# A second whole ring tile at the first block's end, more raw tiles around topk, and the last norm of blocks 2 and 3 written ahead of the gathered block's last selection

## The chip, the cores and the metric

One Trainium2 chip, one core of it. The metric is the device time of one execution in microseconds; lower is better. The times shown are of separate executions on the chip, the median of three.

## What is computed

One layer on 512 tokens of width 2048, all in float32: a mixer of a chunked mLSTM and a forgetting attention with a common output projection, a cross attention to 256 memory rows, and a PEER feed-forward, each with a residual and a layer norm. The reference, cut to what the change touches:

```python
def reference(x, mem, ...):
    h = hybrid_mixer(x, w_in, ..., w_out)
    x = layer_norm(DN_ALPHA * x + h, ln_w[0], ln_b[0])
    h = memory_cross_attention(x, mem, w_xq, w_xkv, w_xo)
    x = layer_norm(DN_ALPHA * x + h, ln_w[1], ln_b[1])
    h = peer_ffn(x, peer_wq, peer_sub_keys, peer_u, peer_v)
    return layer_norm(DN_ALPHA * x + h, ln_w[2], ln_b[2])

def peer_ffn(x, w_pq, sub_keys, expert_u, expert_v):        # cut
    q = (x @ w_pq).reshape(B, S, 8, 2, 128)
    sc = einsum('bshpd,hpnd->bshpn', q, sub_keys)           # two times 128 scores a head
    top_s, top_i = top_k(sc, 16)
    ...                                                     # the best 16 of 16 x 16 sums
    idx, g = ..., softmax(best_s)                           # 128 experts of 16384 for each token
    a = einsum('tkd,td->tk', expert_u[idx], x)
    return einsum('tk,tkd->td', gelu(a) * g, expert_v[idx])
```

## The kernel before

**Blocks.** The tokens are cut in four blocks of 128. Block 0 goes through the mixer alone, blocks 1 to 3 together. After the mixer, block 1 (e1 in the code) and blocks 2 and 3 (e2, two blocks at once) go their own ways through attention and norms. In the PEER part blocks 0 and 1 take the gathered way: a selection (Choice) finds the 128 experts of each token, their rows are gathered by GpSimd's indirect DMA, and VectorE multiplies them in (job_u, line 1027, and job_v, line 1043, one instruction of 128x2048 a job, 256 jobs a block). Blocks 2 and 3 take the dense way: all 16384 experts are multiplied, and a gate matrix G, zero but for the chosen experts, masks them.

**Weights, raw tiles and the ring.** Every weight arrives as a raw tile of 128x2048 floats (1 MB), loaded by SP (load_raw, line 158) from a list of pools in turn (raws["pools"]; two buffers of a pool, one for a pool named "one"). A float32 product is made of float32r parts: ScalarE casts the raw tile to its high part (line 179, two casts of 128x1024), VectorE subtracts it for the low part (line 182), and both land in a ring tile that TensorE reads. With one ring tile it is used as two halves: a cast, a subtract of 128x1024, and the matmuls of half a raw. With two or more, a whole tile is filled at a time (subtract of 128x2048). The second is added while the first block runs (pool wx) and taken away at that block's end; another is added (pool w2) when the mixer of blocks 1 to 3 is done. Lines 201, 243, 244 and 251 are the matmuls of group_ws and group_as that read the ring.

**What sets the order.** The program is written as generators that mix() weaves together, so many steps of one for a step of the other; a scheduler with its own timeline then sets the final order on each engine. Engines run their rows in order, SP's transfers among them.

**Jobs.** Each subtract of the ring is a tick. It adds rate x cost x mult to a credit (at most 2.0), and each whole unit starts one job: the gather is issued, and its VectorE product is placed "lag" ticks later. The rate is set as the jobs left divided by a number (980 for block 1's 256 jobs). The cost is 4.2 for a uT tile and 4 for most others there. mult is 0.7 until topk ends, then 1.3, and 1.0 in main.

**The stretches that the change touches**, in the order of the program:

- The end of the first block: its norm, attention, residual with Bv, second norm and selection (pool pick0) are woven with the first groups of the mLSTM of blocks 1 to 3 (ml1). The ring has one tile in halves here.
- pick1: block 1's selection, woven with the attention of e2 (att). A selection has four groups; a group multiplies by peer_wq, evaluates scores (line 983), copies them (985) and runs select on VectorE (lines 900 to 942); soften (950 to 953) follows the last, and indices writes ei and gg (993, 994), on which the gathers wait. Then block 1's jobs are added, and the second residual (lines 758, 759) and norm of e2 follow: the sum of the statistics (767), rstd (267 to 273), line 770, the scaling on ScalarE (777), PE's transposes (787), and the splits Xh and Xl (147, 148).
- topk: the selection of blocks 2 and 3, eight selects, woven with next_a. One next_a loads a tile of uT, multiplies it by the tokens (lines 1263, 1266, 1270) and, for each pair, applies gelu (ga).
- gbuild: the selections are transposed (line 1304), G is built (L1322 is its matmul) and written to DRAM (gd), with one next_a in every second step.
- The tail of look-ahead: next_a until LOOK tiles are done (64). A pair too far ahead to be kept is spilled to DRAM (gad).
- main: stage_o multiplies vD tiles (lines 1374, 1375, 1383) by hp, the product of G (line 1341 reads it from gd, line 1344 the spilled ga from gad, on SP) and gelu; next_a goes on inside it until all 128 tiles of uT are done. In its second part a third raw tile (pool main) is used.

## Time and profile before

| | us |
|---|---|
| median of 3 executions | 4734.93 (4732.48 to 4737.19) |
| the profiled execution's own time | 4737.65 |
| span of the profiled execution | 4736.0 |
| TensorE busy | 4501.5 |
| VectorE busy | 3766.3 |
| ScalarE busy | 2239.5 |
| GpSimd busy | 885.8 |

The mean granted clock of TensorE is 0.98. The stretches above lie in the trace as follows, counted from the span's start: the first block's end 947 to 1245 us, the last part of pick1 and e2's residual 2850 to 2958, its norm to 3000, topk to 3264, gbuild to 3470, the look-ahead to 3611, and main to 4716. A window's row gives its busy time by engine; a busy TensorE may still run at a lowered clock, so the granted clock is read beside it. A wait's row reads "engine line waited for <- engine line that released it: total us, times, longest". A matmul's listed duration overlaps with its neighbours', so the pace is read from the starts.

### The profile page before, as it was taken

To read this page: it belongs to the slowest core of one execution; us is meant where nothing else is said; L and a number is where in the kernel's file an instruction comes from. 1 tells how busy PE (TensorE), PEld (TensorE's weight loads), DVE (VectorE), ACT (ScalarE), POOL (GpSimd) and SP (SyncE) were. 2 spreads that over 40 slices of the span, in tenths; PEclk is the share of its full clock that TensorE was granted. 3 is DMA by queue.
4 is the path that set the end of the run, shared out by engine and by line. 5 is a ranking of instruction groups with operands and counts; after the bars stand their busy time and mean duration, and the time that the engine had idled before them with its cause. 6 is when DMAs were issued, how large, how long until landed. Compare 5 with 4: busy or idle time off the path is not lost.

```text
span 4736.0 us, 65181 instructions
## 1 busy us (share of the span) xinstructions
PE 4501.5 (95%) x25662; PEld 4001.0 (84%) x25662; DVE 3766.3 (80%) x4276; ACT 2239.5 (47%) x3043; POOL 885.8 (19%) x631
## 2 busy tenths in 40 slices
PE   8999999988999999999999988998979999999998
PEld 6888888888888899999898776898867778888887
DVE  7876777556888877888788669899868998888885
ACT  6766776544334423333323674435743433343333
POOL 1000000000122222222121000212223123333320
PEclk9999999999999999999999999999989999999999
DMA  7899888655798888888699765777899999999994
GB/s 286 323 332 329 321 321 332 226 198 202 272 342 325 333 325 348 333 335 319 257 347 340 261 224 197 290 299 273 333 357 365 409 393 387 379 381 380 381 376 152
DMA packets 260628, 1489.76 MB, mean 315 GB/s; under 512 B 27068, under 2 KB 69116, under 8 KB 91744
## 3 DMA queue, kind: packets, MB, share of 16 engines
q1 hardware_dynamic: 167280, 890.04, 50.6%
q0 software_dynamic: 81664, 561.95, 30.7%
q10 hardware_dynamic: 11376, 33.59, 1.8%
q8 instruction: 201, 3.29, 0.3%
q14 instruction: 107, 0.88, 0.0%
HBM read 1426.72 MB, written 58.76 MB: 314 GB/s over the span
## 4 chain that ended last, share of the span: by engine, by line
PE 59%; DVE 11%; DMA 6%; ACT 3%; issue 2%; ACTq 0%; DVEq 0%; SPq 0%
PE mm L201 19%; PE mm L244 5%; PE mm L243 5%; PE mm L251 5%; DVE ring L182 5%; PE mm L1383 4%; PE mm L1374 4%; PE mm L1375 3%; PE pa L1270 3%; PE pa L1263 3%; PE pa L1266 3%; DVE rows L1027 1%; ACT ring L179 1%; DMA raw<-in_uT 1%; DMA rows<-in_peer_u,ei 1%
## 5 line engine op out<-in xcount | busy, mean ns | idle before, releaser
L179 ACT CAST ring<-raw 128x1024 fp32r<-128x1024 f32 x1568 | 1597.9, 1050 | 1726.6 <-PE mm L201 463.4
L182 DVE TENSOR_TENSOR ring<-raw,ring 128x2048 fp32r<-128x2048 f32 (+1 forms) x968 | 1818.2, 1882 | 586.1 <-ACT ring L179 267.3
L1007 POOL DMA_INDIRECT rows<-in_peer_u,ei x256 | 385.7, 1507 | 1665.6 <-DVE rows L1027 641.6
L201 PE MATMUL mm<-Ah,ring 128*128 128x384 f32 x2560 | 675.3, 343 | 22.5 <-ACT ring L179 12.2
L1007 POOL DMA_INDIRECT rows<-in_peer_v,ei x256 | 433.4, 1693 | 957.2 <-DVE x2l L1043 740.3
L1043 DVE SCALAR_TENSOR_TENSOR x2l<-rows,dots,x2l 128x2048 f32<-128x2048 f32 x256 | 600.4, 2345 | 10.5 <-DMA rows<-in_peer_v,ei 10.1
L1027 DVE SCALAR_TENSOR_TENSOR rows<-rows,x2l 128x2048 f32<-128x2048 f32 x256 | 583.3, 2283 | 27.0 <-DMA rows<-in_peer_u,ei 27.0
L1263 PE MATMUL pa<-Xh,ring 128*128 128x256 f32 x2048 | 504.4, 287 | 48.1 <-ACT ring L179 47.9
L1266 PE MATMUL pa<-Xl,ring 128*128 128x256 f32 x2048 | 499.9, 284 | 0.0
L201 PEld LDWEIGHTS mm<-Ah,ring 128*128 128x128 f32 x2560 | 466.7, 190 | 31.6 <-ACT ring L179 15.7
L1263 PEld LDWEIGHTS pa<-Xh,ring 128*128 128x128 f32 x2048 | 393.5, 192 | 55.5 <-ACT ring L179 53.1
L201 PE MATMUL mm<-Al,ring 128*128 128x384 f32 x1280 | 433.8, 343 | 0.3 <-DVE Al L148 0.3
L1374 PE MATMUL mm<-ring,hph 128*128 128x512 f32 x1024 | 405.2, 396 | 11.3 <-ACT ring L179 10.2
L1375 PE MATMUL mm<-ring,hpl 128*128 128x512 f32 x1024 | 402.7, 394 | 0.0
L1266 PEld LDWEIGHTS pa<-Xl,ring 128*128 128x128 f32 x2048 | 394.2, 192 | 2.1
L243 PE MATMUL mm<-ring,Zh 128*128 128x512 f32 x832 | 328.6, 395 | 5.8 <-ACT ring L179 5.8
L244 PE MATMUL mm<-ring,Zl 128*128 128x512 f32 x832 | 328.9, 395 | 0.0
L243 PE MATMUL mm<-ring,Ah 128*128 128x512 f32 x768 | 306.9, 400 | 1.1 <-ACT ring L179 1.1
L244 PE MATMUL mm<-ring,Al 128*128 128x512 f32 x768 | 304.1, 396 | 0.0
L1270 PE MATMUL pa<-Xh,ring 128*128 128x256 f32 x2048 | 267.2, 283 | 6.8 <-DVE ring L182 6.5
L201 PE MATMUL mm<-Bh,ring 128*128 128x384 f32 x1024 | 262.4, 338 | 4.9 <-ACT ring L179 4.2
L1383 PE MATMUL mm<-ring,hph 128*128 128x512 f32 x1024 | 258.8, 394 | 8.1 <-DVE ring L182 8.1
(388 smaller groups left out, 7100.4 us busy)
## 6 DMA issues: line engine op xcount, KB each, us to landing
raw<-in_w_in SPq DMA_DIRECT2D x256, 1024.0 KB, 6.9
raw<-in_uT SPq DMA_DIRECT2D x128, 1024.0 KB, 7.2
raw<-in_vD SPq DMA_DIRECT2D x128, 1024.0 KB, 9.1
raw<-in_w_out SPq DMA_DIRECT2D x48, 1024.0 KB, 5.7
raw<-in_peer_wq SPq DMA_DIRECT2D x48, 1024.0 KB, 4.9
raw<-in_w_xkv SPq DMA_DIRECT2D x32, 1024.0 KB, 6.6
raw<-in_w_br_ml SPq DMA_DIRECT2D x32, 1024.0 KB, 7.1
raw<-in_w_br_fx SPq DMA_DIRECT2D x32, 1024.0 KB, 6.6
```

Of the source, the lines that this page charges most:

```text
L179: x = nc.scalar.copy(hi[:, c:c + 1024], src[:, c:c + 1024])
L182: s = nc.vector.tensor_sub(lo, src, hi.bitcast(F32))
L201: i = nc.tensor.matmul(o, w, x, start=start and s % per == 0, stop=stop and s % per == per - 1)
L243: nc.tensor.matmul(banks[t], xh[:, tt], wh[:, c], start=k == 0, stop=False)
L244: nc.tensor.matmul(banks[t], xl[:, tt], wh[:, c], start=False, stop=False)
L1007: i = nc.gpsimd.indirect_dma_start(out=rows, out_offset=None, in_=I[table], in_offset=bass.IndirectOffsetOnAxis(ap=ei[t][:, k:k + 1], axis=0))
L1027: i = nc.vector.scalar_tensor_tensor(rows, rows, 1.0, tok[t]["x2l"], op0=ALU.mult, op1=ALU.mult, accum_out=d[:, k % GB:k % GB + 1])
L1043: i = nc.vector.scalar_tensor_tensor(acc, rows, d[:, GB + k % GB:GB + k % GB + 1], acc, op0=ALU.mult, op1=ALU.add)
L1263: i = nc.tensor.matmul(bank, uh[:, sl], xh, start=k == 0, stop=False)
L1266: nc.tensor.matmul(bank, uh[:, sl], xl, start=False, stop=False)
L1374: nc.tensor.matmul(banks[t][g], a[:, tt], vh[:, gs_], start=c == c0, stop=False)
L1375: nc.tensor.matmul(banks[t][g], b[:, tt], vh[:, gs_], start=False, stop=False)
```

## The change

It has five parts.

1. **Ring.** A third ring tile (pool wr0) is added when fx0 of the first block has closed. At that block's end only the tile of wx goes, so that from ml1's first groups to the end of pick0 two whole ring tiles stand where one in halves did. After pick0 the added one goes. Choice takes a "lean" form there (one buffer less each of keysT, qT and sc), and in Ends the rows of x share three "f" buffers with the norm, where "row" had two and "f" two.
2. **Block 1's last selection.** pick1 is run by hand: 15 steps with the attention woven in, then the rest of the attention, then the residual of e2 woven with the last five steps, then its norm, and behind it the last select and soften. Adding block 1's jobs moves behind all of that; the mult after it is 0.5, which was 0.7.
3. **Raw tiles.** From that point a second pool (rw) and in topk a single one (gap) bring the raw tiles to five, two from rw and one from gap beside wp's two. From gbuild on there are three (wp and gap), where there were two until the second part of main and three from there.
4. **topk and gbuild.** In topk's eighth step five next_a run in place of seven; the other two stand behind the copies of the first transposed selection in gbuild.
5. **LOOK** is 68, which was 64: four more uT tiles are multiplied ahead of main, and 28 pairs are spilled, which were 26.

```diff
--- before.py
+++ after.py
@@ -42,7 +42,7 @@
 
 J = 16
 GB = 8
-LOOK = 64
+LOOK = 68
 GA = 7
 MIX = 4
 
@@ -169,7 +169,7 @@
             for i in range(1 if wide else 2):
                 ring["n"] += 1
                 if wide:
-                    t = ring["tiles"][ring["n"] % 2]
+                    t = ring["tiles"][ring["n"] % len(ring["tiles"])]
                     hi, lo, src = t[:, 0:2048], t[:, 2048:4096], raw
                 else:
                     t, o = ring["tiles"][0], (ring["n"] % 2) * 1024
@@ -749,7 +749,7 @@
                 for g in range(4):
                     def ev(t, b, g=g):
                         if first:
-                            xr = self.t("row", 2)
+                            xr = self.t("f", 3)
                             rows = slice((self.b0 + t) * P, (self.b0 + t + 1) * P)
                             self.ld.dma_start(xr, I["x"][rows, g * 512:(g + 1) * 512])
                             r[t][g] = self.rp.tile([P, 512], F32, tag="r", bufs=4 * nb, name=nm("r"))
...
@@ -888,8 +888,8 @@
 
         class Choice:
 
-            def __init__(self, pl, tp, nb):
-                self.tp, self.nb = tp, nb
+            def __init__(self, pl, tp, nb, lean=False):
+                self.tp, self.nb, self.lean = tp, nb, lean
                 self.sel = {n: [pl.tile([P, P], F32, tag=f"{n}{t}", name=nm(f"sel_{n}{t}")) for t in range(nb)]
                             for n in ("i0", "i1")}
                 self.gates = pl.tile([P, nb, P], F32, tag="g2", name=nm("sel_g"))
@@ -956,14 +956,14 @@
                 tp, nb = self.tp, self.nb
                 for g in range(4):
                     qT = {}
-                    ks = tp.tile([P, 4, P], F32, tag="keysT", bufs=2, name=nm("keysT"))
+                    ks = tp.tile([P, 4, P], F32, tag="keysT", bufs=2 - self.lean, name=nm("keysT"))
                     ld.dma_start(ks, I["keysT"][:, 4 * g:4 * g + 4])
 
                     def ev_q(b, bank, qT=qT):
-                        t = tp.tile([P, 512], F32, tag="qT", bufs=3, name=nm("qT"))
+                        t = tp.tile([P, 512], F32, tag="qT", bufs=3 - self.lean, name=nm("qT"))
...
@@ -1108,6 +1108,8 @@
                 yield from ml0(mp, hT, m0)
             with pool("fx0") as fp:
                 yield from fx0(fp, yT, m0, G0)
+            e["wr"] = ExitStack()
+            add_ring(e["wr"].enter_context(pool("wr0")))
             e["xs"] = ExitStack()
             e["x"] = Ends(e["xs"].enter_context(pool("xa0")), 0, 1, nc.gpsimd, nc.gpsimd)
             yield from e["x"].residual(G0, I["w_out"], True)
@@ -1134,7 +1136,7 @@
             mix(e["x"].attend(X1, pr0, PT), ms, 1)
             drain(ms)
         wx.close()
-        del raws["pools"][1:], ring["tiles"][1:]
+        del raws["pools"][1:], ring["tiles"][1]
         ms_.close()
 
         big = ExitStack()
@@ -1177,9 +1179,11 @@
         e["xs"].close()
         take(ml, 2)
         with pool("pick0") as pp:
-            c = Choice(pp, pp, 1)
+            c = Choice(pp, pp, 1, True)
             mix(c.run(X2, nc.gpsimd), ml, 2)
             c.indices(0)
+        del ring["tiles"][1:]
+        e["wr"].close()
         r0s.close()
         gat["pool"] = ctx.enter_context(pool("gat"))
         hp_.append(bs.enter_context(pool("bigB")))
@@ -1223,19 +1227,29 @@
         take(att, 2)
         with pool("pick1") as pp:
             c = Choice(pp, pp, 1)
-            mix(c.run(X2b, nc.sync), att, 5)
+            cr = c.run(X2b, nc.sync)
+            for i in range(15):
+                next(cr)
+                if i % 5 == 4:
+                    take(att, 1)
+            drain(att)
+            cs.close()
+            fpl = ctx.enter_context(pool("x2c", side="right"))
+            mix(e2.residual(PTc, Bv, False), (next(cr) for _ in range(5)), 1)
+            e2.norm(1, X2, lambda: pair(fpl, "X", 16), True)
+            next(cr, 0)
             c.indices(1)
-        drain(att)
-        cs.close()
-        fpl = ctx.enter_context(pool("x2c", side="right"))
+        pre = ExitStack()
+        pp = pre.enter_context(pool("pre", side="right"))
+        rws = ExitStack()
+        rw = rws.enter_context(pool("rw", side="right"))
+        raws["pools"] = [wp, rw]
         while state["done"] < len(jobs):
             raise RuntimeError(f"{len(jobs) - state['done']} jobs left")
         add_jobs(1)
         state["lag"] = 2
         set_rate(980.0)
-        state["mult"] = 0.7
-        drain(e2.residual(PTc, Bv, False))
-        e2.norm(1, X2, lambda: pair(fpl, "X", 16), True)
+        state["mult"] = 0.5
         xs.close()
         bb.close()
 
@@ -1277,17 +1291,18 @@
                 else:
                     gas[c // 2] = ga
 
-        pre = ExitStack()
-        pp = pre.enter_context(pool("pre", side="right"))
+        raws["pools"], raws["one"] = [wp, rw, wp, rw, gap], gap
         with pool("topk", side="right") as tp:
             c = Choice(pp, tp, 2)
             steps = 0
             for w in c.run(X2, nc.sync):
                 if w:
                     steps += 1
-                    for _ in range(7 if steps == 8 else 3):
+                    for _ in range(5 if steps == 8 else 3):
                         next_a(w[1])
         sel = c.sel
+        rws.close()
+        raws["pools"] = [wp, gap, wp]
         state["mult"] = 1.3
 
         def o_bank():
@@ -1304,6 +1319,9 @@
                 nc.tensor.transpose(bank[:, j * P:(j + 1) * P], sel[n][t], ident)
             for j, n in enumerate(("i0", "i1", "g")):
                 nc.vector.tensor_copy(selT[n][:, tt], bank[:, j * P:(j + 1) * P])
+            if t == 0:
+                next_a()
+                next_a()
             for half in range(2):
                 stage = [gp.tile([P, 64, 64], F32, tag="stage", bufs=3, name=nm("stage")) for _ in range(2)]
                 for q in range(16):
@@ -1355,8 +1373,6 @@
         def stage_o(c0, dh, fill):
 
             banks = [[o_bank() for g in range(2)] for t in range(HB)]
-            if c0 == 0 and dh:
-                raws["pools"], raws["one"] = [wp, mn, wp], mn
             for jj in range(J // 2):
                 raw = load_raw(I["vD"][c0 // 2 + jj, dh])
                 for vh, vl, o, w in shares(raw, 2.0):
```

Line numbers behind the changes move by 14 to 18: next_a's 1263, 1266 and 1270 are 1277, 1280 and 1284 after, 1304 is 1319, 1322 is 1340, 1341 and 1344 are 1359 and 1362, 1374 is 1390.

**VectorE at the first block's end.** The rows where the residual of the first block (758, 759) meets ml1's first groups; ring_105 is the ring tile that is always there. Before:

```order
L182 TENSOR_TENSOR ring_105<-raw_7876,ring_105 128x1024 x2
L182 TENSOR_TENSOR ring_105<-raw_7894,ring_105 128x1024 x2
L758 SCALAR_TENSOR_TENSOR r_6278<-r_6278,mm_7875 128x512
L759 BN_STATS rst_7874<-r_6278 128x6
L182 TENSOR_TENSOR ring_105<-raw_7914,ring_105 128x1024 x2
L148 TENSOR_TENSOR Al_7921<-raw_7918,Ah_7920 128x384
L148 TENSOR_TENSOR Al_7925<-raw_7918,Ah_7924 128x384
L148 TENSOR_TENSOR Al_7929<-raw_7918,Ah_7928 128x384
L148 TENSOR_TENSOR Al_7933<-raw_7918,Ah_7932 128x384
```

After, at the same place (ring_6206 is the tile of wr0):

```order
L182 TENSOR_TENSOR ring_6206<-raw_7878,ring_6206 128x2048
L182 TENSOR_TENSOR ring_105<-raw_7895,ring_105 128x2048
L758 SCALAR_TENSOR_TENSOR r_6282<-r_6282,mm_7877 128x512
L759 BN_STATS rst_7876<-r_6282 128x6
L182 TENSOR_TENSOR ring_6206<-raw_7914,ring_6206 128x2048
L148 TENSOR_TENSOR Al_7922<-raw_7919,Ah_7921 128x384
L148 TENSOR_TENSOR Al_7926<-raw_7919,Ah_7925 128x384
L148 TENSOR_TENSOR Al_7930<-raw_7919,Ah_7929 128x384
L148 TENSOR_TENSOR Al_7934<-raw_7919,Ah_7933 128x384
```

Each raw had two subtracts into halves of one tile; it has one into a whole tile, and two tiles take turns.

**VectorE at block 1's last selection and the norm of e2.** rst is the norm's statistics, sel, eq, s and ef are the selection's, gg and ei its results, Xl the splits behind the norm, and rows in L1027 are gathered. Before:

```order
L953 TENSOR_TENSOR sel_g_21552<-sel_g_21552,s_22285 128x128
L939 TENSOR_REDUCE sel_i_2348_21550<-eq_22276 128x32
L770 SCALAR_TENSOR_TENSOR rst_22317<-rst_22317 128x2
L994 COPY gg_104<-sel_g_21552 128x128
L937 TENSOR_TENSOR eq_22280<-pf_22274,iota 128x512
L938 TENSOR_TENSOR eq_22280<-eq_22280,ixf_22253 128x512
L939 TENSOR_REDUCE sel_i_2349_21551<-eq_22280 128x32
L991 SCALAR_TENSOR_TENSOR ef_22290<-sel_i_2348_21550,sel_i_2349_21551 128x128
L993 CAST ei_102<-ef_22290 128x128
L148 TENSOR_TENSOR Xl_22612<-f_22608,Xh_22611 128x512
L1027 SCALAR_TENSOR_TENSOR rows_22356,dots_22424<-rows_22356,x2l_22354 128x2048
L148 TENSOR_TENSOR Xl_22624<-f_22620,Xh_22623 128x512
```

After:

```order
L939 TENSOR_REDUCE sel_i_2349_21513<-eq_22688 128x32
L994 COPY gg_104<-sel_g_21515 128x128
L272 TENSOR_SCALAR rst_22067<-rst_22067 128x2
L937 TENSOR_TENSOR eq_22692<-pf_22686,iota 128x512
L273 TENSOR_TENSOR rst_22067<-rst_22067 128x2
L938 TENSOR_TENSOR eq_22692<-eq_22692,ixf_22665 128x512
L770 SCALAR_TENSOR_TENSOR rst_22067<-rst_22067 128x2
L939 TENSOR_REDUCE sel_i_2350_21514<-eq_22692 128x32
L991 SCALAR_TENSOR_TENSOR ef_22702<-sel_i_2349_21513,sel_i_2350_21514 128x128
L993 CAST ei_102<-ef_22702 128x128
L148 TENSOR_TENSOR Xl_22490<-f_22486,Xh_22489 128x512
L148 TENSOR_TENSOR Xl_22502<-f_22498,Xh_22501 128x512
```

In both, the selection's steps and the norm's alternate up to L770, which stands 21 rows behind the sum of the statistics (L767) in both; the copy gg stands ahead of L770 now, one reduction (L939) behind it. The L1027 between the Xl are gone: the first stands seven rows after the last row shown.

**SP at the end of the look-ahead.** uT and vD are raw tiles, G reads gd, gb reads gad, acc reads the residual of blocks 2 and 3. Before:

```order
L158 DMA raw_27944<-in_uT 128x2048
L158 DMA raw_28040<-in_uT 128x2048
L1341 DMA G_28984<-gd 128x4x128
L1341 DMA G_29023<-gd 128x4x128
L1368 DMA acc_28732<-x2d 128x2048
L1341 DMA G_29063<-gd 128x4x128
L1368 DMA acc_28733<-x2d 128x2048
L1344 DMA gb_29225<-gad 128x512
L1344 DMA gb_29266<-gad 128x512
L158 DMA raw_29337<-in_vD 128x2048
L1344 DMA gb_29582<-gad 128x512
L158 DMA raw_28126<-in_uT 128x2048
```

After:

```order
L158 DMA raw_28585<-in_uT 128x2048
L158 DMA raw_28659<-in_uT 128x2048
L158 DMA raw_28715<-in_uT 128x2048
L158 DMA raw_28776<-in_uT 128x2048
L1359 DMA G_29138<-gd 128x4x128
L1359 DMA G_29177<-gd 128x4x128
L1384 DMA acc_28656<-x2d 128x2048
L1359 DMA G_29217<-gd 128x4x128
L1384 DMA acc_28657<-x2d 128x2048
L1362 DMA gb_29382<-gad 128x512
L1362 DMA gb_29423<-gad 128x512
L1362 DMA gb_29739<-gad 128x512
```

Before, eleven uT tiles of the look-ahead stand behind the first G; now five do, and the ten rows ahead of the first G are all uT.

More of the change, by code (lines that the diff above doesn't have):

```diff
@@ L788, in norm @@
                                                     r[t][g][:, s * P:(s + 1) * P], ident)
-                        f = self.t("f", 2)
+                        f = self.t("f", 3)
                         for c in range(cpb):
@@ L958, in run @@
                     qT = {}
-                    ks = tp.tile([P, 4, P], F32, tag="keysT", bufs=2, name=nm("keysT"))
+                    ks = tp.tile([P, 4, P], F32, tag="keysT", bufs=2 - self.lean, name=nm("keysT"))
                     ld.dma_start(ks, I["keysT"][:, 4 * g:4 * g + 4])
                     def ev_q(b, bank, qT=qT):
-                        t = tp.tile([P, 512], F32, tag="qT", bufs=3, name=nm("qT"))
+                        t = tp.tile([P, 512], F32, tag="qT", bufs=3 - self.lean, name=nm("qT"))
                         nc.scalar.copy(t, bank)
                         if nb == 1:
-                            u = tp.tile([P, 512], F32, tag="qT", bufs=3, name=nm("qT"))
+                            u = tp.tile([P, 512], F32, tag="qT", bufs=3 - self.lean, name=nm("qT"))
                             nc.scalar.copy(u, turn4(t))
@@ L983, in run @@
                             nc.tensor.matmul(bank[:, j * P:(j + 1) * P], w, ks[:, j], start=True, stop=True)
-                        sc = tp.tile([P, 512], F32, tag="sc", bufs=2, name=nm("sc"))
+                        sc = tp.tile([P, 512], F32, tag="sc", bufs=2 - self.lean, name=nm("sc"))
                         yield "s", nc.scalar.copy(sc, bank)
```

## The prediction

> **What bounds the kernel now.** I read the page first, then a table of windows, then the waits inside the windows that the change touches.
>
> ```profile
> PE 4501.5 (95%) x25662; PEld 4001.0 (84%) x25662; DVE 3766.3 (80%) x4276; ACT 2239.5 (47%) x3043; POOL 885.8 (19%) x631
> PE 59%; DVE 11%; DMA 6%; ACT 3%; issue 2%; ACTq 0%; DVEq 0%; SPq 0%
> ```
>
> These are the busy times and the engines' shares of the chain that ended last. TensorE bounds the kernel as a whole, so a change can win only where PE idles or its clock is cut. The windows say where. Columns: stretch, its us, then busy us and count for PE, weight load, DVE, ACT and POOL, then granted clock, DMA share and GB/s.
>
> ```profile
> 947.00:1245.00 298.00, 269.43 (x1376) 244.91 (x1375) 189.51 (x406) 132.36 (x167) 6.73 (x12) 0.96 0.56 195
> 2850.00:2958.00 108.00, 87.46 (x397) 70.62 (x395) 107.31 (x276) 49.91 (x65) 0.00 (x0) 0.94 0.51 186
> 2958.00:3000.00 42.00, 35.44 (x264) 33.76 (x264) 28.04 (x31) 28.29 (x48) 8.54 (x8) 0.86 0.81 301
> 3000.00:3264.00 264.00, 241.63 (x1978) 236.80 (x1978) 259.10 (x583) 97.24 (x114) 51.03 (x31) 0.98 0.77 293
> 3264.00:3470.00 206.00, 187.45 (x1503) 184.47 (x1504) 186.81 (x216) 159.49 (x437) 47.33 (x27) 0.94 0.80 309
> 3470.00:3611.00 141.00, 99.71 (x744) 97.44 (x744) 93.50 (x81) 41.99 (x56) 38.72 (x21) 0.85 0.97 370
> 3611.00:3900.00 289.00, 279.83 (x1184) 220.55 (x1184) 260.39 (x216) 112.65 (x128) 80.48 (x49) 0.99 1.00 392
> 3900.00:4570.00 670.00, 663.06 (x4193) 595.01 (x4191) 582.96 (x321) 263.27 (x290) 240.85 (x120) 1.00 0.98 382
> 4570.00:4716.00 146.00, 141.70 (x766) 121.82 (x767) 89.04 (x65) 59.77 (x62) 5.16 (x2) 0.98 0.60 227
> ```
>
> The first row is stage A, from the end of the first block to the gathered block's first selection (one ring tile in halves). The next two are stage B (last selection of block 1, residual and norm of blocks 2 and 3). 3000 to 3264 is C (topk), 3264 to 3611 is D (gbuild and the up-products ahead of main), the rest main and its tail. Main is full: 663 of 670 at clock 1.00. A, B, C and D are not, and each has another limit: A the ring, B and C VectorE (107 of 108, 259 of 264), D transfers.
>
> **A: wide ring.** Who keeps ScalarE, which fills the ring, waiting in A (total, times, longest):
>
> ```profile
> ACT ring L179 <- PE mm L201: 64.0, 26, 4.3
> ACT ring L179 <- DMA raw<-in_w_in: 25.3, 9, 4.0
> ACT ring L179 <- PE mm L244: 15.9, 16, 4.7
> ACT ring L179 <- DMA raw<-Bd: 12.2, 4, 4.6
> ACT ring L179 <- DMA raw<-in_peer_wq: 8.8, 3, 4.0
> ```
>
> The casts wait 79.9 us for a ring half that PE still reads, and 46.3 us for a raw. The change removes the first kind in the main: a second whole tile stands ready. No row of A shows the new form, but the kernel uses it later, with the same two raws. Those 150 us:
>
> ```profile
> 2600.00:2650.00 50.00, 50.00 (x217) 40.27 (x216) 34.26 (x22) 29.12 (x29) 0.00 (x0) 1.00 0.84 302
> 2650.00:2700.00 50.00, 47.37 (x212) 37.89 (x211) 31.27 (x31) 30.41 (x46) 0.00 (x0) 0.97 0.66 240
> 2700.00:2750.00 50.00, 47.64 (x206) 38.19 (x205) 33.68 (x27) 31.89 (x43) 0.00 (x0) 0.98 0.69 256
> ```
>
> A loses 298 - 269.43 = 28.6 us to idling and 0.04 x 298 = 11.9 to the clock: 40.5. The later stretch loses 5.0 and 0.017 x 150 = 2.5; scaled by 298/150 that is 14.9. The gain is 40.5 - 14.9 = **26 us**. The upper end is 36 (only some 4 us lost). The lower is below nothing, where raws bind: halves free a raw after two casts and a short subtract, a whole tile after two casts and a long one.
>
> ```profile
> L182 DVE TENSOR_TENSOR ring<-raw,ring 128x1024 fp32r<-128x1024 f32 x91 | 110.4, 1219 | 94.1 <-PE mm L201 50.2 <-ACT ring L179 36.5 <-ACT r L807 2.7
> L182 DVE TENSOR_TENSOR ring<-raw,ring 128x2048 fp32r<-128x2048 f32 x40 | 91.1, 2278 | 3.7 <-ACT ring L179 3.6
> ...
> PE mm L201 <- ACT ring L179: 12.2, 8, 2.2
> ```
>
> The raw is free 2.278 - 1.219 = 1.06 us later (first row A, second C), half of that for each of 45 raws since two take turns: -24. I take 26, since the later stretch has the form itself.
>
> PE's own waits in A are short, 2.2 us at most on the last line, and yet the clock there is 0.96. The Trainium skill, "TensorE: Matmul & The Clock Gate", section "HAM oscillation — how this bites in real kernels", holds that gaps above about 3.4 us are those that cut the clock. By it these waits would not have cost clock, and A would gain the idle part alone, 28.6 - 9.9 = 19 us; the two granted clocks (0.96 and 0.983) speak for 26.
>
> The same part's smaller edits: a third ring tile during the first block's w_out residual and attention, where PE is already near full, one buffer less each for keys, queries and scores in that selection, and the x rows in one tag with the norm's tile. They add no instruction. The selection's scores are read by VectorE, which has 108 us to spare in A; if that cover goes, four waits for the scores of a few us are the price. I take 0, ends -3 and +3.
>
> **B: norm placed ahead of the selection.** PE's wait for the norm and the chain before it:
>
> ```profile
> PE sm L787 <- ACT r L777: 17.2, 1, 17.2
> ...
> 2957.06 0.07 DVE rst L273
> ...
> 2957.33 0.60 DVE sel_i L939
> 2957.93 0.08 DVE rst L770
> ```
>
> The wait is PE's largest here, and the norm's last step (L770) stands behind the selection's steps on a VectorE that is busy 107.3 of 108 us. By intent the norm now comes first. The order rows shown with the change say otherwise: the two are still woven, L770 stands 21 rows behind the statistics' sum (L767) now as it did, and only the copy of the gates and a few steps change sides. VectorE is full, and has the same work ahead of L770 as before; PE has the same matmuls ahead of L787, in another order. So the wait stays about what it is. I take **0**, and for the ends half the wait, -8 and +8.
>
> What does go are the gathers: add_jobs now stands behind residual and norm, so the eight that POOL issued by 3000 wait, and seven products L1027 leave the splits Xl there. PE's loss in those 42 us is 6.6 and not from them in the main; 0 to 2, inside B's ends.
>
> **C: topk.** VectorE binds, 259.10 of 264. The price of a product with gathered rows (a subtract's stands above):
>
> ```profile
> L1027 DVE SCALAR_TENSOR_TENSOR rows<-rows,x2l 128x2048 f32<-128x2048 f32 x30 | 68.3, 2278 | 0.0
> ```
>
> Each converted raw adds rate x cost x mult to a credit, one job for each whole unit; the rate is 256/980 = 0.261. With 0.7 a raw of 4.2 gave 0.77 jobs, with 0.5 it gives 0.55. Counting through, 39 jobs are granted by the end of topk before (POOL's x8 + x31 in the windows), 22 now, when the residual's eight tiles give none. Eight of the 17 stood in B; nine leave C: 9 x 2.28 = 20.5 us of VectorE. Two tiles of uT move behind the first transposes, so two subtracts (4.6 us) go as well. The whole is 25; the last jobs and subtracts lie behind the last selection's end in part. I take **18**, ends 5 and 25. PE, with 241.6 - 2 x 5.7 = 230 us, does not take over before VectorE at 239. Five raw tiles in flight instead of two only help here.
>
> **D: gbuild and look-ahead.** What PE waits for, SP's issues in the gap, and the transfer that PE needed:
>
> ```profile
> PE pa L1263 <- ACT ring L179: 38.3, 10, 18.5
> ...
> 3478.72 0.33 SPq L158 DMA_DIRECT2D raw<-in_uT  x1
> 3485.17 2.50 SPq L1341 DMA_DIRECT2D G<-gd  x2
> 3489.25 9.53 SPq L1341 DMA_DIRECT2D G<-gd  x1
> 3504.42 11.12 SPq L158 DMA_DIRECT2D raw<-in_uT  x2
> ...
> 3504.42 20.03 DMA raw<-in_uT
> ```
>
> SP works in order: the reads of G stand there until the last writes of gd have landed, and the next uT tile behind them is issued only at 3504.4. Two tiles that were in flight are used up, PE stops for 18.5 us. In the new order ten more uT tiles stand ahead of the first G. That gap and one of 8.7 should go. But D has more to do: two tiles from C, four by LOOK 68. One tile costs PE
>
> ```profile
> 3475.83 0.28 PE L1263 MATMUL pa<-Xh,ring 128*128 128x256 f32 x1
> 3475.95 0.28 PE L1266 MATMUL pa<-Xl,ring 128*128 128x256 f32 x1
> ```
>
> 48 matmuls started 0.12 us apart, 5.7 us; six cost 34. PE's present loss in D is (206 - 187.45) + (141 - 99.71) = 59.8 idle and 0.06 x 206 + 0.15 x 141 = 33.5 of clock, so work of 347 - 93 + 34 = 288 us at full pace. The transfers bind instead. Bytes of the two halves, and two landings:
>
> ```profile
> DMA packets 8946, 63.69 MB, mean 309 GB/s; under 512 B 992, under 2 KB 992, under 8 KB 2272
> DMA packets 15648, 52.23 MB, mean 370 GB/s; under 512 B 1087, under 2 KB 8767, under 8 KB 10431
> rows<-in_peer_u,ei POOLq DMA_INDIRECT x27, 9.1
> rows<-in_peer_v,ei POOLq DMA_INDIRECT x113, 10.8
> ```
>
> To 115.9 MB come six tiles, and seven gathers (by the credit 86 - 39 = 47 jobs are granted in D before, 76 - 22 = 54 now), of 1.05 MB each: 129.6. At 370 GB/s, the second half's rate, D takes 350 us; at main's 392, 331; at D's present mean, 115.9/347 = 0.334 MB/us, 388. The four tiles of LOOK leave main, which is PE bound: 4 x 5.7 = 22.6 back. So D with main's relief is worth 347 - 350 + 22.6 = **20 us**, ends 347 - 388 + 22.6 = -18 and +39. I take 370, the rate where D was fed. In "DMA: Bandwidth & Descriptors", section "Issuing engines are not separate DMA queues", the Trainium skill has transfers of all issuers share the same 16 engines; the DMA shares of 0.97 to 1.00 agree, and by it a third raw in flight buys no rate beyond 392.
>
> **Main and tail.** The put-off jobs end 19 ticks before the last raw, not 32; those lie in the stretch 4570 to 4716 with DMA at 0.60, VectorE at 89 of 146 us. Cost 0 to 4; I take 2. Third raw: main had three already.
>
> **Sum**, against the profiled run's 4737.65 us (span 4736.0, 1.65 outside, 2.7 above the median of the three): 26 + 0 + 18 + 20 - 2 = 62, giving **4676**.
>
> **The rivals.**
>
> *The bytes take it back.* Jobs leave a stage with DMA share 0.77 for stages at 0.97 to 1.00; D then runs at its present mean and gives -18. A 26, C 18, tail -2: 4737.65 - 24 = 4714. For it: the shares. Against: D's low mean is made by gaps in which uT wasn't issued.
>
> *In A raws bind, not tiles.* The 46 us of waits for raws grow by what the tiles give up; A gives 0: 4702. For it: two raws only, and Bd and peer_wq waits. Against: the 150 us of the same form, also on two raws. A slower A (-24) gives 4726.
>
> *B does what its words say.* If the last selection did stay behind the norm, the wait shrinks by 8 to 17 us: 4659 to 4668. Against: the order.
>
> *Slower.* From gbuild on a third raw flies beside gathers and G. If gathers land later than their lag of two ticks, VectorE, in order, stops at L1027 with ring subtracts behind it, and PE waits for these. It decides from a landing of 2 x 5.7 = 11.4 us; 2 us beyond that for the 54 jobs of D is 108 us: 4676 + 108 = 4784. For it: 9.1 us in D on two raws, 10.8 in main on three. Against: at 10.8 main kept PE at 99%.
>
> **How the numbers follow.** Forecast 0.54, bytes 0.18, raws in A 0.14, B's words 0.06, slower 0.08. The low end is A, C and D at their upper ends together, 36 + 25 + 39 - 2 = 98: 4640. The high end is A at its lower end, 4726, which takes in the bytes' 4714. Left out are the slower case and sums of several lower ends, 0.15 to 0.2. Between runs of this kernel 0.2% (9.5 us) is about what a measurement can tell from no change. Faster by over that (below 4725): 0.54 + 0.06 and, of the bytes and the raws, all but 0.06, so 0.86; within it 0.06; slower 0.08.
>
> **What would show it.** Right: PE near 283 of 298 us in A's span and casts waiting for raws instead of tiles; the 17 us wait of L787 still there; the topk selections ending about 18 us sooner, counted from L770, with some 22 gathers issued; no PE gap above 5 us at the first G reads; D at 370 GB/s or above. Wrong: waits of L1027 for rows above 50 us in D, ACT waiting over 90 us for raws in A, or D's rate still near 334.

## The result and the profile after

The changed kernel takes 4692.69 us, the median of four executions (4692.06 to 4698.4), against 4733.7 for the kernel before (4729.88 to 4737.19): the ratio is 0.9917 with a 95% interval of 0.9902 to 0.9932. It is faster by 0.8%, some 41 us, where 59 below the median of before were forecast.

The busy times on the page of the changed kernel:

```profile
PE 4466.1 (95%) x25662; PEld 3986.0 (85%) x25662; DVE 3764.6 (80%) x4234; ACT 2233.0 (48%) x3040; POOL 894.8 (19%) x631
```

TensorE has lost 35 us of busy time with the same 25662 matmuls, and its mean granted clock is 0.983, which was 0.980, so part of the gain lies in the clock. Windows of the changed kernel, cut at its own landmarks (columns as in the prediction's table):

```profile
944.00:1219.00 275.00, 260.32 (x1382) 241.59 (x1381) 185.79 (x360) 129.48 (x169) 5.38 (x10) 0.98 0.61 213
2771.00:2927.00 156.00, 130.39 (x591) 104.36 (x589) 135.32 (x315) 88.37 (x131) 0.00 (x0) 0.94 0.57 209
2927.00:2968.00 41.00, 35.48 (x264) 34.02 (x264) 13.52 (x18) 28.53 (x48) 3.68 (x2) 0.85 0.59 219
2968.00:3201.00 233.00, 219.53 (x1820) 216.54 (x1821) 223.20 (x525) 92.80 (x106) 32.55 (x20) 1.00 0.66 251
3201.00:3456.00 255.00, 243.64 (x2018) 240.38 (x2017) 237.91 (x276) 181.63 (x465) 56.16 (x36) 0.99 0.89 342
3456.00:3550.00 94.00, 74.02 (x582) 73.00 (x580) 63.55 (x55) 32.35 (x43) 20.88 (x13) 0.91 1.01 401
3550.00:4540.00 990.00, 972.10 (x5555) 849.54 (x5556) 879.77 (x580) 393.40 (x441) 344.95 (x172) 1.00 0.98 388
4540.00:4670.00 130.00, 82.98 (x396) 69.08 (x396) 84.43 (x57) 31.06 (x32) 19.51 (x13) 0.82 0.66 254
```

The last row was full before (141.70 of 146 in the tail's window) and is now the worst of these: PE works 83 of 130 us. The first block's end, topk, gbuild and the look-ahead run fuller than before; the two rows of stage B (2771 to 2968) run as they did. PE's largest wait of the whole execution lies in the last row, among the waits from 4500 us on:

```profile
PE mm L1390 <- ACT ring L179: 48.6, 2, 47.0
```

The stages between landmarks, each time taken from the starts in the two traces (first ei: first result of a selection for the jobs; norm: last execution of line 770; first up-product: the first matmul of next_a; G and vD: the first products of gbuild and main):

| stretch, us | before | after | gain | forecast |
|---|---|---|---|---|
| start to the first ei (A) | 1241.9 | 1218.0 | 23.9 | 26 |
| to the last norm | 1715.9 | 1708.7 | 7.2 | 0 |
| to the first up-product | 43.0 | 41.7 | 1.3 | 0 |
| to the first transposed selection (C) | 253.8 | 232.2 | 21.6 | 18 |
| to the first vD product (D) | 356.1 | 349.7 | 6.4 | -3 |
| first to last vD product (main) | 1103.6 | 1118.2 | -14.6 | 20.6 |

The forecast of D and main is that of the term for D (350 us in place of 347, then four tiles of main's 22.6 us) and the tail's -2. The stages sum to 45.8, the spans differ by 45.6 (4736.0 and 4690.4). These are single traces. This trace and seven of the experiments' have the same program up to the first ei, and put it at 1218.0 to 1222.6 us, so A's gain is 19 to 24 us. In the seven of these whose program is the same up to the last norm, that norm comes at 2925.7 to 2933.7. Differences of a few us between two traces mean little.

**The gap in the tail.** Three views of the changed kernel. First SP's issues (start, length, what), then VectorE in the gap (with the idle time before a row in brackets):

```profile
4540.15 23.79 SPq L158 DMA_DIRECT2D raw<-in_vD  x5
4594.59 0.33 SPq L1064 DMA_DIRECT2D lw<-in_ln_w  x1
4597.02 0.33 SPq L1064 DMA_DIRECT2D lw<-in_ln_b  x1
4600.17 5.71 SPq L158 DMA_DIRECT2D raw<-in_vD  x2
```

```profile
4567.84 2.35 DVE L1043 SCALAR_TENSOR_TENSOR x2l<-rows,dots,x2l 128x2048 f32<-128x2048 f32 x1 [1.56 <-DMA rows<-in_peer_v,ei]
4572.40 4.78 DVE L1043 SCALAR_TENSOR_TENSOR x2l<-rows,dots,x2l 128x2048 f32<-128x2048 f32 x2 [2.22 <-DMA rows<-in_peer_v,ei]
4578.70 2.35 DVE L1043 SCALAR_TENSOR_TENSOR x2l<-rows,dots,x2l 128x2048 f32<-128x2048 f32 x1 [1.52 <-DMA rows<-in_peer_v,ei]
```

SP issues nothing from 4564 to 4594.6. The norm's weights (lw) of the gathered block stand next, and they are loaded into two of the three row buffers, the buffers of the gathered rows, which the last gathers still use. Behind lw stands a vD tile, and load_raw has a rule for it: when all jobs have been granted for more than six raw tiles, each second raw tile goes into a row buffer too. That tile waits for the third buffer, and it is the one that PE needs next. VectorE meanwhile has no ring subtract to do and works through the last products as their rows land. The chain of waits through the same stretch:

```profile
4588.69 0.94 POOL rows L1007
4589.63 1.46 issue
4591.32 6.38 DMA rows<-in_peer_v,ei
4597.79 2.36 DVE x2l L1043
4600.17 6.92 DMA raw<-in_vD
4607.11 1.05 ACT ring L179
```

Before, at the same place, lw stood among vD and uT tiles in turn, and four other vD tiles had been issued from 4558 us on:

```profile
4585.12 0.33 SPq L1064 DMA_DIRECT2D lw<-in_ln_w  x1
4589.94 0.33 SPq L158 DMA_DIRECT2D raw<-in_vD  x1
4592.21 0.33 SPq L1064 DMA_DIRECT2D lw<-in_ln_b  x1
4594.50 0.33 SPq L158 DMA_DIRECT2D raw<-in_vD  x1
4596.76 0.33 SPq L158 DMA_DIRECT2D raw<-in_uT  x1
```

and PE's largest wait from 4540 us on was this:

```profile
PE mm L1374 <- ACT ring L179: 4.3, 1, 4.3
```

In the changed kernel the last job comes when only vD tiles are left to load (the last uT tile is issued at 4531.5 us). That this is what lets the gap open is not shown: jobs_early and mult07 below have a gap with uT tiles left.

### The profile page after: what moved, and what is told of

The parts are those of the page before. It is cut to its first block, busy times and chain, and to the rows that moved or that the text cites. A ratio compares the mean times of both kernels' runs of the same rounds, so it can differ in the third digit from the quotient of the medians.

```text
span 4690.4 us, 65123 instructions
## 1 busy us (share of the span) xinstructions
PE 4466.1 (95%) x25662; PEld 3986.0 (85%) x25662; DVE 3764.6 (80%) x4234; ACT 2233.0 (48%) x3040; POOL 894.8 (19%) x631
## 5 line engine op out<-in xcount | busy, mean ns | idle before, releaser
L1007 POOL DMA_INDIRECT rows<-in_peer_v,ei x256 | 443.9, 1734 | 929.3 <-DVE x2l L1043 696.6
L1027 DVE SCALAR_TENSOR_TENSOR rows<-rows,x2l 128x2048 f32<-128x2048 f32 x256 | 582.7, 2284 | 22.0 <-DMA rows<-in_peer_u,ei 21.8
L1277 PE MATMUL pa<-Xh,ring 128*128 128x256 f32 x2048 | 499.8, 285 | 32.3 <-ACT ring L179 16.8
L201 PEld LDWEIGHTS mm<-Ah,ring 128*128 128x128 f32 x2560 | 463.6, 189 | 20.6 <-ACT Ah L147 7.4
L1390 PE MATMUL mm<-ring,hph 128*128 128x512 f32 x1024 | 405.5, 396 | 63.0 <-ACT ring L179 62.6
L1390 PEld LDWEIGHTS mm<-ring,hph 128*128 128x128 f32 x1024 | 193.9, 189 | 109.0 <-ACT ring L179 67.3
```

What stands on the lines that cost most here:

```text
L201: i = nc.tensor.matmul(o, w, x, start=start and s % per == 0, stop=stop and s % per == per - 1)
L1007: i = nc.gpsimd.indirect_dma_start(out=rows, out_offset=None, in_=I[table], in_offset=bass.IndirectOffsetOnAxis(ap=ei[t][:, k:k + 1], axis=0))
L1027: i = nc.vector.scalar_tensor_tensor(rows, rows, 1.0, tok[t]["x2l"], op0=ALU.mult, op1=ALU.mult, accum_out=d[:, k % GB:k % GB + 1])
L1277: i = nc.tensor.matmul(bank, uh[:, sl], xh, start=k == 0, stop=False)
L1390: nc.tensor.matmul(banks[t][g], a[:, tt], vh[:, gs_], start=c == c0, stop=False)
```

## The experiments

Each ratio is to the kernel before, run beside the experiment on the same chip, where its median was 4727.0 to 4730.1 us. The first four experiments took up the gap.

**Raw tiles kept out of the row buffers, everywhere** (tail_pools, on the changed kernel):

```diff
-            if raws["idle"] > 6 and raws["n"] % 2:
+            if raws["idle"] > 600 and raws["n"] % 2:
```

> The changed kernel, but late raw tiles never take one of the gathers' three row buffers. Theory (a vD tile that PE needs next waits on SP behind the gathered block's norm weights, both for row buffers that the last gathers still hold): the 47 us gap of PE near 4560 us goes, PE's longest wait after 4500 us is under 10 us, and the time is 4645 to 4665. Rival (the last gathers themselves land late and VectorE, in order, stands at their products): a gap of over 25 us stays and the time is 4675 or more.

It took 4700.02 us, ratio 0.9943 (0.9926 to 0.9959). The gap is gone, PE's longest wait there is 3.4 us and main takes 1075.5 us. But the last norm comes at 2972.9 instead of 2926.7, so the forecast time was missed and the time is near that of the changed kernel. The rule works also between the end of block 0's jobs and the start of block 1's, and there it adds the three row buffers to the two raw tiles. ScalarE's largest waits from 2400 us to the last norm in tail_pools:

```profile
ACT ring L179 <- PE mm L201: 71.7, 25, 7.1
ACT ring L179 <- DMA raw<-in_w_out: 71.1, 25, 6.3
ACT ring L179 <- DMA raw<-Bd: 29.1, 13, 4.4
```

and in the changed kernel, in the same stretch:

```profile
ACT ring L179 <- PE mm L201: 89.1, 31, 7.1
ACT ring L179 <- PE mm L244: 68.7, 53, 8.1
ACT ring L179 <- DVE ring L182: 27.2, 14, 3.2
```

With the rule the casts wait for ring tiles; without it they wait for raws, of which there are two (157.8 us over all weights, 22.0 with the rule). So one edit undid a loss and made another of the same size.

**More jobs per tick in main** (jobs_early):

```diff
-        state["mult"] = 1.0
+        state["mult"] = 1.2
```

> The changed kernel with mult 1.2 in place of 1.0 in main, so that the last job is granted about 20 ticks sooner and late raw tiles in row buffers are uT tiles again, as before the change. Theory: the gap near the end goes and the time is 4645 to 4670. Rival (main is held by the bytes of the gathers, so more of them per tick slow it as much): 4685 or more, without a gap of 40 us but with PE's idle time in main up by 30 us.

4753.97 us, ratio 1.0055 (1.0038 to 1.0071): slower than before the change. The theory is wrong; the rival has the time but said that there would be no gap. The gap has grown and moved. PE's waits in main:

```profile
PE pa L1277 <- ACT ring L179: 102.1, 3, 100.3
```

and SP's issues:

```profile
4429.85 40.27 SPq L158 DMA_DIRECT2D raw<-in_vD  x8
4556.32 0.33 SPq L1064 DMA_DIRECT2D lw<-in_ln_w  x1
4561.72 5.71 SPq L158 DMA_DIRECT2D raw<-in_uT  x2
```

It is the same queue, now with a uT tile behind lw, and SP stands for 86 us. When SP stops, 24 gathers are still to be issued (8 in the changed kernel). They pass the three buffers one after another, one every 3.5 us. The last product does end sooner, at 4561.7 us instead of 4600.1, but lw stands so much further ahead of it on SP that what is queued behind lw waits longer.

**mult as before in topk** (mult07), and **LOOK as before** (look64):

```diff
-        state["mult"] = 0.5
+        state["mult"] = 0.7
```

> The changed kernel with mult 0.7 in topk as before, all else as changed. Theory (the put-off jobs brought topk its gain and the tail its gap): topk from the first up-product to the first transposed selection is 12 to 22 us longer than the changed kernel's 232, the gap near the end is gone or under 10 us, and the time is 4660 to 4675. Rival (the put-off jobs have nothing to do with the gap): the gap stays and the time is 4705 to 4715.

4699.96 us, 0.9938 (0.9922 to 0.9955), between the two expectations. Topk takes 252.8 us to the first transposed selection, 20.6 more than the changed kernel and 1.0 less than before. To the third it takes 261.4 us, 251.3 in the changed kernel and 263.4 before. By either count the jobs put off are most of C's gain. Of the gap this is left:

```profile
PE pa L1277 <- ACT ring L179: 25.7, 1, 25.7
```

So later jobs make the gap larger, but even at 0.7 it doesn't go. Which other part of the change makes the rest was not tried; with the ring's part alone (ring_only below) PE's longest wait there is 2.5 us.

```diff
-LOOK = 68
+LOOK = 64
```

> The changed kernel with LOOK 64 as before, all else as changed. Theory (the gap at the end comes from jobs that end late, not from up-products that end early): the gap stays at 35 us or more, and the time is 4685 to 4705. Rival (LOOK 68 lets the up-products end early and so puts vD tiles into the row buffers): the gap goes and the time is 4650 to 4670.

4693.48 us, 0.9924 (0.9907 to 0.994), as the theory said: PE's longest wait in main is 48.2 us. D is 26.2 us shorter (323.5) and main 28.7 us longer (1146.9). LOOK moves work from one stage to the other and gains nothing.

**The rule put off in main alone** (tail_main, on the changed kernel):

```diff
-            if raws["idle"] > 6 and raws["n"] % 2:
+            if raws["idle"] > 6 and raws["n"] % 2 and "main" not in raws:
...
         hs = {}
+        raws["main"] = 1
         state["mult"] = 1.0
```

> The changed kernel, but in main alone late raw tiles never take one of the gathers' row buffers (before main they do, as in the changed kernel). Theory: all up to main stands as in the changed kernel, the 47 us gap goes as it did in tail_pools, main (first to last vD matmul) takes 1072 to 1080 us in place of 1118, and the time is 4645 to 4656. Rival (tail_pools lost its 46 us before main by chance of the schedule, not by the two raw tiles that it lacks there): the time is again near 4700.

4649.43 us, ratio 0.9827 (0.981 to 0.9845): faster than both kernels. Main takes 1071.5 us, and PE's largest waits in it are

```profile
PE mm L1391 <- ACT ring L179: 15.6, 10, 2.6
PE mm L1400 <- DVE ring L182: 4.3, 5, 1.5
```

SP's issues show why. The twelve vD tiles go out one after another, and lw comes last:

```profile
4544.16 60.17 SPq L158 DMA_DIRECT2D raw<-in_vD  x12
4614.35 0.33 SPq L1064 DMA_DIRECT2D lw<-in_ln_w  x1
```

This shows the gap's cause, since the program is the changed kernel's row for row up to lw on SP and up to the last 187 of PE's 25662 matmuls. What differs is the order of the tail alone: a vD tile that shares lw's buffers stands behind lw, and one that doesn't goes ahead of it.

**The same on the kernel before** (before_tail):

> The kernel before with late raw tiles kept out of the row buffers in main, as in tail_main. Theory (the gap is made by the change's later jobs): before has no such gap, so the time is within 8 us of before. Rival (the rule costs before as well, spread over many small waits): 15 us or more faster than before.

4725.11 us, 0.9989 (0.9979 to 1.0), as the theory said. Main takes 1095.9 us against 1103.6. The rule's large cost came with the change; before, it cost a few us.

The other parts, one by one. **The ring's part alone** (ring_only: the third ring tile, the lean selection and the shared f buffers on the kernel before, as in the change's diff):

> The kernel before with the ring's part alone: third ring tile, lean selection, shared f buffers. Theory: block 1's first experts' numbers (ei of the first selection) come 22 to 26 us sooner than before, and the time is 4705 to 4715 against 4735. The norm of e2 tells whether the further 8 us that the changed kernel had won there belong to this part (then its last norm comes 30 to 33 us sooner) or to the rest (22 to 26).

4702.89 us, 0.9944 (0.9926 to 0.9962). The first ei comes at 1220.5, 21.4 us sooner than before, the last norm 31.9 us sooner. This first selection is that of the first block, block 0; the expectation calls it block 1's. Both the ei and the time lie just outside what was expected. So all that the change gains up to the norm, 31.1 us, is in this part, though only 19 to 24 of it in A. For the rest the shared buffers were tried next.

**Shared f buffers alone** (f_row, on the kernel before):

```diff
-                            xr = self.t("row", 2)
+                            xr = self.t("f", 3)
...
-                        f = self.t("f", 2)
+                        f = self.t("f", 3)
```

> The kernel before with the shared f buffers alone (x rows and the norm's tile, three of one tag). Theory (the 8 us that ring_only wins between block 1's first job results and the last norm are this edit's): that stretch, first ei to the last L770, is 6 to 9 us shorter than before's 1715.9, and the time is 4720 to 4728 on a chip where before takes 4730. Rival (they come with the ring's earlier release or by the schedule): the stretch stays within 3 us.

4717.09 us, 0.9965 (0.9951 to 0.9979), a little faster than forecast. First ei to last norm takes 1707.5 us, 8.4 less, and A is as long as before (1242.0). From the first of e1's norms to the last norm it is 6.0 of them, 273.7 us against 279.7. Of the 8.4, some may be chance: before_tail, whose program is the kernel before's up to the tail of main, takes 1711.0 and 278.3. So these two lines are worth some 4 to 8 us there, and how the third buffer saves them was not tried apart. The time gained is 13 us, more than this stretch holds; the rest was not traced. Nor do they explain the changed kernel's 7.2 us: its norms' stretch is 278.4 us, and some 6 of the 7.2 lie ahead of it.

**The selection in the old order** (pick1_old, on the changed kernel):

```diff
-            cr = c.run(X2b, nc.sync)
...
+            mix(c.run(X2b, nc.sync), att, 5)
+            c.indices(1)
+        drain(att)
...
+        drain(e2.residual(PTc, Bv, False))
+        e2.norm(1, X2, lambda: pair(fpl, "X", 16), True)
```

> The changed kernel with block 1's last selection, the rest of the attention, the residual and the norm in the old order; the jobs are still added behind the norm. Theory (the new order changes nothing that VectorE does ahead of the norm): PE's wait for the scaling stays 14 to 20 us and the last norm's factor comes within 5 us of the changed kernel's 2926.7. Rival (the new order wins by itself and something else loses as much): the norm comes 8 us or more later.

4684.95 us, 0.9905 (0.9884 to 0.9927). The norm's factor comes at 2925.4 us against 2926.7, as the theory said. The new order wins nothing there, and may cost some 3 us: from the first of e1's norms to the last norm it takes 274.6 us here and 277.4 to 279.8 in the seven traces with the new order. PE's longest wait for the scaling is 17.1 us here, 17.2 before, and in the changed kernel

```profile
PE sm L787 <- ACT r L777: 16.8, 1, 16.8
```

**Two raw tiles in topk** (topk_raws2, on the changed kernel):

```diff
-        raws["pools"] = [wp, rw]
+        raws["pools"] = [wp]
...
-        raws["pools"], raws["one"] = [wp, rw, wp, rw, gap], gap
+        raws["pools"], raws["one"] = [wp], gap
```

> The changed kernel with two raw tiles in topk as before, in place of five. Theory (VectorE binds topk, the jobs put off are its gain): the stretch from the first up-product to the first transposed selection stays within 5 us of the changed kernel's 232. Rival (the raw tiles are the gain): it goes back by 12 us or more, towards 254. ScalarE's waits for raws there are above the changed kernel's in both.

4689.79 us, 0.9915 (0.9897 to 0.9933). The stretch to the first transposed selection is 222.1 us, 10 shorter, which neither expectation has, and to the third it is 254.6, 3 longer. ScalarE's waits for raws are 56.3 us here and none in the changed kernel, and yet five raw tiles bring next to nothing.

**On the free tail.** With the gap away, two parts could be weighed on tail_main. First mult 0.7 again (tail_main_m7):

> tail_main with mult 0.7 in topk as before. Theory (VectorE in topk pays for each job, main takes put-off jobs for nothing once the tail is free): the third transposed selection comes 8 to 14 us later than in tail_main, main is as long, and the time is 4655 to 4665. Rival (put-off jobs are paid in main at the same price): the time is 4649 within 5.

4670.4 us, 0.9871 (0.985 to 0.9892), 21 us above tail_main. The third transposed selection comes 262.8 us after the first up-product, 11.9 more, as expected. Main is 11.8 us longer (1083.3), which neither expectation has. PE's waits differ by only a few us, but the granted clock of main is 0.99, and 1.00 in tail_main: four short stretches, 17 us in sum, ran at 0.50, each at a wait of 2.0 to 3.0 us. tail_main has no such stretch. That is 8.5 of the 11.8 us; the rest, and why these waits arise, stays open. Putting jobs off pays in topk and is not paid back in main.

Then two raw tiles from gbuild to main's second part (tail_main_g2):

```diff
-        raws["pools"] = [wp, gap, wp]
+        raws["pools"] = [wp]
...
             banks = [[o_bank() for g in range(2)] for t in range(HB)]
+            if c0 == 0 and dh:
+                raws["pools"] = [wp, gap, wp]
```

> tail_main with two raw tiles from gbuild to the second part of main, as before, in place of three. Theory (the earlier uT issues and the third raw tile carry stage D): from the first G product to the first vD product it takes 336 to 350 us in place of 324, and the time is 4660 to 4675. Rival (the order alone carries it, the third tile buys nothing on full transfers): within 5 us of 324, time 4645 to 4655.

4690.75 us, 0.9923 (0.9895 to 0.9951), 41 us above tail_main. From the first G product to main it takes 363.6 us in place of 323.7, more than either expectation. PE's largest wait there, 3.8 us in sum in tail_main:

```profile
PE pa L1277 <- ACT ring L179: 40.3, 13, 12.9
```

and the windows of gbuild and look-ahead, here and, in the last two rows, in tail_main:

```profile
3226.00:3458.00 232.00, 210.56 (x1704) 206.63 (x1703) 204.09 (x220) 163.48 (x439) 61.53 (x33) 0.96 0.86 332
3458.00:3576.00 118.00, 85.22 (x633) 83.61 (x634) 80.15 (x71) 36.50 (x47) 28.76 (x16) 0.86 0.95 360
3230.00:3461.00 231.00, 224.10 (x1858) 221.46 (x1859) 215.85 (x229) 173.22 (x453) 54.41 (x34) 0.99 0.88 341
3461.00:3554.00 93.00, 72.61 (x581) 71.59 (x579) 63.21 (x55) 32.36 (x43) 22.72 (x13) 0.91 1.02 403
```

With the third raw tile the look-ahead moves 403 GB/s, with two 360 (370 in the kernel before). In gbuild the rates are close, 341 and 332, but PE works 224.10 of 231 us in place of 210.56 of 232. The third tile carries D's gain.

## Why the prediction was right, and where it was not

**Right in sign and range; the sum was too large** by some 16 us. Main and tail were 35 us worse than forecast, C and D together 13 better and the stretch up to the last norm 5 better, and that these partly cancel was luck.

*A.* 26 forecast, 23.9 measured (21.4 with the part alone, 19 to 24 over eight traces). The casts' waits turned from tiles to raws as written:

```profile
ACT ring L179 <- DMA raw<-in_peer_wq: 37.5, 11, 6.9
ACT ring L179 <- DMA raw<-in_w_in: 30.8, 11, 6.2
ACT ring L179 <- DMA raw<-Bd: 21.9, 7, 4.2
ACT ring L179 <- PE mm L201: 16.8, 8, 3.1
```

Raws take 90.2 us now, 46.3 before; on PE's side it hardly shows (260 of 275 us busy). By the sign I had set at 90 us this would have counted as wrong, and the sign was badly chosen: ScalarE's waits cost only what reaches PE. The stretch that I took for the form of A had the three row buffers beside its two raws, not two raws alone as the prediction says; tail_pools showed what they are worth. The analogy was worse than I thought, and that the number survived it was luck. Of the rival of the raws the condition came (waits for raws grew by 44 us while those for tiles fell by 56), but not its result, an A that gains nothing.

On the clock, idle time gave 28.6 - 14.7 = 13.9 us and the granted clock 11.9 - 0.02 x 275 = 6.4. The prediction's "2.2 us at most" holds for the line that it quotes, but another line of the same window has longer waits:

```profile
PE mm L201 <- ACT Ah L147: 7.9, 3, 3.7
```

In the trace before, the granted clock is 0.50 for 6.8 us behind each of the two longest waits, 3.6 and 3.7 us, and for 3.4 us behind three of 2.0 to 2.3 us. The Trainium skill ("TensorE: Matmul & The Clock Gate", section "HAM oscillation — how this bites in real kernels") accounts for the first two and not for the other three, which are 10 of the 24 us; there the measurement decides.

*The part costed at nothing.* Shared f buffers, ends -3 and +3: f_row measures 4 to 8 us of the stretch and 13 of the median, which is outside these ends. The prediction put no price on the waits of the norms, which are short each (3.1 us at most on PE in the e1 and e2 norms' window before).

*B.* 0 forecast, -1 to 1 measured. The wait that stays, 16.8 us, and the same wait in the old order of pick1_old show that the written order doesn't set it; that VectorE's load does is argued from its busy time.

*C.* 18 forecast, 21.6 measured to the first transposed selection. The prediction's stage ended at the third (3264 us), and to there it is 12.1. The count of jobs held: 22 gathers are issued by the first transposed selection, 39 before. mult07 gives most of the gain back, and the raw tiles had little share in it.

*D.* Forecast 350 us, and the table has 349.7, but that is luck: the table counts from the first transposed selection, the prediction from the third. From there D takes 330.5 us and had taken 346.5, so D is 16 us better than before and 19.5 better than the term. The rate was 356 GB/s, below the 370 of the term and of the sign, and the bytes were 117.5 MB in place of 129.6: from the third selection on 37 uT tiles were issued, 34 before, where six more were counted, and 46 gathers, where 54 were. The prediction's "a third raw in flight buys no rate beyond 392" nearly held (401 in the look-ahead). It missed that two tiles don't keep the transfers at that rate, and what the third is worth, 40 us in tail_main_g2. PE's waits of 18.5 and 8.7 us for raws ahead of G went, but the sign "no PE gap above 5 us at the first G reads" failed, since another wait came there, for gelu results (ga):

```profile
PE pa L1277 <- ACT ga L1288: 15.4, 2, 9.0
```

The rival of the bytes was wrong.

*Main and tail: the step that failed.* "Cost 0 to 4; I take 2": main and tail were 35 us off (-14.6 in place of 20.6). The mis-sized term is the tail. I had checked that the shares of DMA and VectorE left room for the late jobs and not who else uses the buffers that these jobs hold. tail_main measures it: 46.7 us of main. The other term held: with the rule off on both sides, before_tail and tail_main, main is 24.4 us shorter, where LOOK's four tiles were put at 22.6. The slower rival, gathers that land beyond their lag, did not come: L1027's waits for rows in D were 16.2 us before and are now, in the changed kernel's waits of VectorE,

```profile
DVE rows L1027 <- DMA rows<-in_peer_u,ei: 10.3, 2, 7.8
```

What did come is a cousin of it, a queue that stands behind a buffer, on SP instead of VectorE.

## What to carry to other kernels

A load that waits for a buffer stops everything behind it on its queue (here SP stood for 31 us, and in jobs_early for 86). So when work is put off to a later stage, follow its buffers to the end and see who shares them, not only the engines' room. And where a rule lends a buffer from one stage to another, take it away stage by stage: here the same rule was worth 46 us in one place and cost 47 in another. Here a third tile in flight paid 40 us in D, where transfers bound but two tiles didn't keep them at their top rate, and more raw tiles paid next to nothing in topk, where VectorE bound.

## What was not expected of the hardware

Two raw tiles beside gathers reached 309 to 332 GB/s in gbuild and 360 to 370 in the look-ahead, three 341 to 342 and 401 to 403. Granting gathers faster made them no faster at the end: with three buffers a gather was issued every 3.5 us, and 20% more jobs per tick turned a wait of 47 us into one of 100. And some waits of only 2.0 to 2.3 us were followed by 3.4 us at half the granted clock.
